# A transformer block on one core: own weight tiles for the last two blocks of the first feed-forward, no GpSimd work in the token mixers, and a re-ordered opening

## The chip, the core and the metric

The kernel runs on one core of a Trainium2 chip. The engines are named as in the profile: PE is TensorE (PEld its weight loads), DVE is VectorE, ACT is ScalarE, POOL is GpSimd, SP is SyncE, which here only issues DMAs. The metric is the device time of one execution in microseconds (us), the median over several runs; lower is better. About 0.2% (2 us) is the smallest change that a measurement of this kernel tells from none.

## What is computed

One layer over 256 latent tokens with 256 context tokens, width 1024, all in float32:

```python
mod = silu(c) @ w_ada + b_ada                  # 9 vectors of 1024 for x, and for ctx with c_ctx
x   = x   + 0.5 * g1x * swiglu(modulate(rmsnorm(x)), w13_ffn1, w2_ffn1)     # d_ff = 2816
ctx = ctx + 0.5 * g1c * swiglu(modulate(rmsnorm(ctx)), w13_ffn1, w2_ffn1)
qc, kc, vc, ...  = modulate(rmsnorm(ctx)) @ w_in
qx, kx, vx, g, f, ga, gf = modulate(rmsnorm(x)) @ w_in
o = bidirectional retention of x, started from the states of ctx             # 4 heads, rope on q, k
r = (silu(g) * (o - mean) * rsqrt(var + eps) * gn_w) @ p_ret
fo = real(fft2(f by groups of 256)) @ p_four
x = x + g2x * ((sigmoid(ga) * r + sigmoid(gf) * fo) @ w_out)
x = x + 0.5 * g3x * swiglu(modulate(rmsnorm(x)), w13_ffn2, w2_ffn2)
return rmsnorm(x)
```

## The kernel before

Data lie transposed: 8 tiles of 128 channels by 512 tokens (columns 0 to 255 are the context, 256 to 511 the latents), two to each of the `xs` tiles. To keep float32 accuracy, each operand of a product is split in a high part (rounded to fp32r) and a low part, and `mm3` (L95 to L97) makes three products: low weight by high data, high by low, high by high. A weight is therefore first loaded raw by a DMA on SP's queue (`wr`, four buffers), then cast by ACT (`wh`, L85), and subtracted by DVE or POOL (`wl`, L86), four buffers each. `load_w` does the three steps; its argument `lo_engine` chooses the engine of the subtraction. Four `t2k` buffers serve most temporaries; there are 8 PSUM banks.

The stages in order:

- The opening (L98 to L415), in an order written out by hand for PE, ACT, DVE and SP. Squares of `xs` are summed by products with a tile of ones (`st`, L257); ACT takes the square root (`sd1q`), DVE the reciprocal (`rstd1q`, L235), and four products with a pick matrix spread it over the partitions (`rs`, L269). DVE's `ada` (L198) makes one column of the modulation from an `ada` weight tile; PE makes another by transposing such a tile (`ada_turn`, L284), multiplying it (`ada_rows`, L295) and turning the row back (`ada_cols`, L306). Then the first three blocks of the up product run over 8 steps `k` (`first_products`), with `first_scaled`, `first_split` and `first_shifted` feeding them.
- The rest of the first feed-forward: `ffn1_up` and `ffn1_down` for two halves of the 22 blocks. In the second `ffn1_down` the last two output blocks, j = 6 and 7, are made for the context first (`y_6_0`, `y_7_0`) and then for the latents (`y_6_1`, `y_7_1`), so that the context's norm (`stage2_norm(0)`, `st_0`, `sd_0`, `rstd_0`) is under way while PE still works. Outside the opening the scheduler of the framework orders each engine's instructions.
- The mixers. `stage2_mod` makes the modulated `h2c` (context) and `h2x` (latents): per block a DVE product (`xr`, L328), an ACT addition with rounding (`h2ch`, L331), and a DVE subtraction (`h2cl`, L332). `first_unit` makes head 0's keys from them while PE transposes them (`ht`, L631); its `hook` starts the latents' norm behind block `HOOK`. Then for each of four heads: scores (`score_unit`), `u_unit`, `o_unit` (with the squares `os`, added on POOL at L757) and `o_norm`. The subtractions of `wk` and `wq` for head 0 and of the first four gate weights `wg` are on POOL.
- The gates: eight `gate_unit`s, with the Fourier branch between them (`fourier_tokens`: `fac`, `fbc`, `cu`; `fourier_channels`: `mx`). `o_norm` of the last head stands behind `gate_unit(1)`; its result, `tt` 6 and 7, is used by `gate_unit(6)` and `gate_unit(7)`.
- The merge, the output product, the second feed-forward and the last norm, which the change does not touch.

Of the kernel before, what the change touches and what calls it, by code (L numbers as in the profile page):

```python
# [13 lines left out]
P = 128  # L14
# [15 lines left out]
HOOK = 0  # L30
# [9 lines left out]
def block_kernel(ctx: ExitStack, tc: tile.TileContext, i: dict, out: bass.AP):  # L40
# [36 lines left out]
    def load_w(src, n, lo_engine=None, at=0):  # L77

        uid[0] += 1
        raw, hi, lo = [wtile(t, f"{t}{uid[0]}")[:, at : at + n] for t in ("wr", "wh", "wl")]  # L80
        dst = raw
        if len(src.shape) == 3:
            dst = dst.rearrange("p (k c) -> p k c", k=src.shape[1])
        nc.sync.dma_start(dst, src)
        S.copy(hi, raw)  # L85
        (lo_engine or V).tensor_tensor(lo, raw, f32(hi), op=ALU.subtract)  # L86
        return hi, lo
# [76 lines left out]
    nc.sync.dma_start(sm, i["smalls"])  # L164
# [76 lines left out]
    for k in range(KT):  # L241
        if k < T2K:
            sq = tp.tile([P, 512], F32, name=f"sq1_{k}", tag="t2k", bufs=T2K)
        else:
            sq = stp.tile([P, 512], F32, name=f"sq1_{k}", tag=f"at{k % 2}" if k < 6 else "xr", bufs=1 + (k > 5))
        if k % 2:
            V.tensor_tensor(sq, xs[k], xs[k], op=ALU.mult)
        else:
            S.activation(sq, xs[k], AF.Square)
        if k == 1:  # L250
            cb_copy(0, V.tensor_copy)
            cb_copy(1, S.copy)
        if k == 3:
            cb_copy(2, V.tensor_copy)
            cb_copy(3, S.copy)
        for q in range(4):
            PE.matmul(  # L257
                ps_st[32 * q : 32 * q + 32, :P], ones[:, :32], sq[:, q * P : (q + 1) * P],
                start=(k == 0), stop=(k == KT - 1), skip_group_check=True, tile_position=(0, 32 * q),
            )  # L260
    pick = stp.tile([P, 512], F32, name="pick")
    V.memset(pick, 0.0)
    for q in range(4):
        V.memset(pick[32 * q : 32 * q + 1, q * P : (q + 1) * P], 1.0)
    r1 = rstd_of(ps_st[:, :P], P, "1q")
    ps_st = bank("rs1")
    rstd1 = stp.tile([P, 512], F32, name="rstd1")
    for q in range(4):
        PE.matmul(  # L269
            ps_st[:, q * P : (q + 1) * P], pick[:, q * P : (q + 1) * P], r1, start=True, stop=True  # L270
        )
    for s in range(2):
        S.copy(rstd1[:, s * T : (s + 1) * T], ps_st[:, s * T : (s + 1) * T])

# [28 lines left out]
    def ada_cols(n):  # L303

        tr, row = turned.pop(n)
        PE.matmul(tr[0][:, :2], row, both, start=True, stop=True)  # L306
        V.tensor_scalar(
            mod[:, :, n : n + 1].rearrange("p s o -> p (s o)"), tr[0][:, :2],
            sm[:, BIAS + n : BIAS + n + 1], None, op0=ALU.add,
        )  # L310

# [44 lines left out]
    def first_split(k):  # L356
        hi, lo = wtile("wh", f"wh0_{k}"), wtile("wl", f"wl0_{k}")
        S.copy(hi[:, :n1], first_w[k][:, :n1])
        V.tensor_tensor(lo[:, :n1], first_w[k][:, :n1], f32(hi[:, :n1]), op=ALU.subtract)
        first_hl[k] = hi, lo  # L360
# [30 lines left out]
    ada_turn(0)  # L391
    first_scaled(0)
    first_split(0)
    ada_rows(0)
    ada_cols(0)
    first_shifted(0)
    acc = [bank(f"acc{m}") for m in range(2 * M1)]
# [45 lines left out]

    def w2_chunks(src, kts, at=0):
# [27 lines left out]
    def ffn1_down(hf, gs, n_ada=0):  # L472
# [3 lines left out]
        for j in range(KT):  # L476
            some_ada(n_ada)
            in_two = hf and j >= KT - 2
            ws = w2_chunks(i["w2a"][hf, j], (6, 5), 16 if in_two else 0)
            if in_two:  # L480
# [81 lines left out]
    nc.sync.dma_start(dist, i["dist"])  # L562
# [19 lines left out]
    nc.sync.dma_start(raw, i["unit"])  # L582
    V.tensor_copy(unit, raw)
    dec = {0: decays(0)}
    S.activation(warm, dec[0][0][:, :1], AF.Sqrt, bias=dec[0][1][:, :1])
    ffn1_down(1, g)
    ffn1.close()
# [104 lines left out]
    def k_weights(hd):  # L692
        return [load_w(i["wk"][hd, n], 1024, None if hd else G) for n in range(2)]
# [28 lines left out]
    def q_weights(hd):  # L722
        return [load_w(i["wq"][hd, n], 1024, None if hd else G) for n in range(2)]
# [21 lines left out]
    def o_unit(hd, us):  # L745
# [8 lines left out]
        sq = [tp.tile([P, 512], F32, name=f"os{hd}_{n}", tag="t2k", bufs=T2K) for n in range(2)]  # L754
        for d in range(4):
            S.activation(sq[d // 2][:, (d % 2) * T : (d % 2 + 1) * T], pss[d][:, :T], AF.Square)
        G.tensor_tensor(sq[0], sq[0], sq[1], op=ALU.add)  # L757
# [3 lines left out]
        return sq[0]  # L761
# [82 lines left out]
    def gate_unit(n):  # L844
        ws = [load_w(i["wg"][n, c], 1024, G if n < 4 else None) for c in range(2)]
# [48 lines left out]
    o_norm(HEADS - 1, sq)  # L894
# [10 lines left out]
    for n in range(5, KT):  # L905
        gate_unit(n)
# [260 lines left out]
```

## Time and profile before

| | |
|---|---|
| runs before | 989.15, 987.53, 987.61 us; median 987.61 |
| profiled execution | 986.11 us, of which the span from first to last instruction is 984.3 |
| granted TensorE clock, mean | 0.995 |
| PE busy | 957.3 us (97%) |
| DVE, ACT, POOL busy | 658.1 (67%), 468.1 (48%), 37.7 (4%) |
| subtractions of 128x1024 on DVE (L86) | 174, 1223 ns each |
| the same on POOL | 12, 2515 ns each |

A profile is one execution. In the timeline a row gives the start, the duration of the group of like instructions that follow each other, engine, line and operation, and in brackets the idle time of the engine ahead of it and what ended that. The table of windows gives the busy time of each engine in a stretch, with the number of instructions, the clock that PE was granted (1.00 is full), the share of the DMA engines and GB/s. A busy PE is not always a fast PE: the granted clock tells more.

### The profile page before, as it was taken

The page shows a single profiled execution, that of the slowest core. Times are in us where ns is not written, and L with a number is a line of the kernel's source. Part 1 is how long each engine was busy: PE and PEld are TensorE (multiplying, and loading weights), DVE is VectorE, ACT ScalarE, POOL GpSimd, SP SyncE. Part 2 cuts the span into 40 slices and gives each one's busy share as a digit, 9 for nine tenths or more (in the row PEclk, how much of TensorE's full clock was granted, in tenths as well). Part 3 has the DMA queues.
Part 4 walks back from the last instruction along what each step waited for, and adds up shares of the span by engine and source line. Part 5 has one row for each costly group of instructions (what it writes and reads, how often), then busy time and mean ns, then how long its engine had stood idle before and what let it go on. Part 6 is the DMA issues. An engine that isn't in the chain of part 4 may idle for free.

```text
span 984.3 us, 16732 instructions
## 1 busy us (share of the span) xinstructions
PE 957.3 (97%) x6792; PEld 881.2 (90%) x6792; DVE 658.1 (67%) x1056; ACT 468.1 (48%) x733; POOL 37.7 (4%) x21
## 2 busy tenths in 40 slices
PE   6999999999999999899999999899999999999996
PEld 4778888888888889899999999899999999999995
DVE  7879999998333433966765646975555688555553
ACT  5444322224422432755665647755444566555541
POOL 0000000000000001200000006200000000000000
PEclk9999999999999999999999999999999999999998
DMA  8757766995332232323231526356656565666661
GB/s 348 238 203 235 235 195 214 352 391 195 97 109 67 78 99 86 97 87 121 95 130 44 157 81 186 117 175 201 192 189 199 174 190 175 211 198 186 199 190 43
DMA packets 49237, 166.84 MB, mean 169 GB/s; under 512 B 5380, under 2 KB 7044, under 8 KB 49160
## 3 DMA queue, kind: packets, MB, share of 16 engines
q1 hardware_dynamic: 49160, 165.77, 52.4%
q8 instruction: 53, 0.87, 0.3%
q14 instruction: 24, 0.20, 0.1%
HBM read 164.70 MB, written 1.05 MB: 168 GB/s over the span
## 4 chain that ended last, share of the span: by engine, by line
PE 93%; DVE 3%; ACT 1%; DMA 1%; issue 1%; DVEq 0%; SPq 0%; ACTq 0%
PE y L95 4%; PE y L97 4%; PE y L96 4%; PE pa L97 4%; PE pb L95 4%; PE pa L95 4%; PE pb L97 4%; PE pa L96 3%; PE pb L96 3%; PE ro L97 2%; PE ro L95 2%; PE ro L96 2%; PE fb L97 2%; PE fa L97 2%; PE fb L96 2%; PE fa L96 2%
## 5 line engine op out<-in xcount | busy, mean ns | idle before, releaser
L86 DVE TENSOR_TENSOR wl<-wr,wh 128x1024 fp32r<-128x1024 f32 (+1 forms) x214 | 248.7, 1163 | 190.4 <-ACT wh L85 189.5
L85 ACT CAST wh<-wr 128x1024 fp32r<-128x1024 f32 (+1 forms) x226 | 227.3, 1007 | 273.7 <-PE y L97 79.2
L198 DVE CUSTOM_DVE_ANT_0 junk<-ada,cb,sm 128x1024 bf16<-128x1024 f32 x96 | 123.0, 1281 | 6.5 <-DMA ada<-in_ada 4.9
L96 PE MATMUL y<-gl,wh 128*128 128x512 f32 (+1 forms) x198 | 72.4, 366 | 0.0
L95 PE MATMUL y<-gh,wl 128*128 128x512 f32 (+1 forms) x198 | 72.3, 366 | 0.0
L97 PE MATMUL y<-gh,wh 128*128 128x512 f32 (+1 forms) x198 | 72.2, 365 | 0.0
L97 PE MATMUL pa<-h1h,wh 128*128 128x512 f32 x152 | 59.2, 389 | 0.0
L96 PE MATMUL pa<-h1l,wh 128*128 128x512 f32 x152 | 59.2, 389 | 0.0
L95 PE MATMUL pa<-h1h,wl 128*128 128x512 f32 x152 | 59.2, 389 | 0.0
L95 PE MATMUL pb<-h1h,wl 128*128 128x512 f32 x152 | 59.2, 389 | 0.0
L96 PE MATMUL pb<-h1l,wh 128*128 128x512 f32 x152 | 59.2, 389 | 0.0
L97 PE MATMUL pb<-h1h,wh 128*128 128x512 f32 x152 | 59.1, 389 | 0.0
L96 PE MATMUL z<-g2l,wh 128*128 128x256 f32 x176 | 48.8, 277 | 0.0
L97 PE MATMUL z<-g2h,wh 128*128 128x256 f32 x176 | 48.6, 276 | 0.0
L95 PE MATMUL z<-g2h,wl 128*128 128x256 f32 x176 | 48.6, 276 | 0.0
L86 POOL TENSOR_TENSOR wl<-wr,wh 128x1024 fp32r<-128x1024 f32 x12 | 29.9, 2515 | 439.2 <-ACT wh L85 439.2
L96 PEld LDWEIGHTS y<-gl,wh 128*128 128x128 f32 x198 | 37.3, 188 | 6.1
L95 PEld LDWEIGHTS y<-gh,wl 128*128 128x128 f32 x198 | 37.2, 188 | 6.0
L97 PEld LDWEIGHTS y<-gh,wh 128*128 128x128 f32 x198 | 37.2, 188 | 6.0
L97 PE MATMUL fb<-hnh,wh 128*128 128x256 f32 x144 | 39.8, 276 | 0.0
L96 PE MATMUL fb<-hnl,wh 128*128 128x256 f32 x144 | 39.8, 276 | 0.0
L97 PE MATMUL fa<-hnh,wh 128*128 128x256 f32 x144 | 39.8, 276 | 0.0
(336 smaller groups left out, 2903.1 us busy)
## 6 DMA issues: line engine op xcount, KB each, us to landing
ada<-in_ada SPq DMA_DIRECT2D x72, 512.0 KB, 5.2
wr<-in_w13b SPq DMA_DIRECT2D x44, 512.0 KB, 4.4
wr<-in_w13a SPq DMA_DIRECT2D x38, 512.0 KB, 4.4
wrv<-in_wv SPq DMA_DIRECT2D x16, 512.0 KB, 4.5
wr<-in_wg SPq DMA_DIRECT2D x16, 512.0 KB, 4.1
wr<-in_wgate SPq DMA_DIRECT2D x16, 512.0 KB, 4.4
wr<-in_pret SPq DMA_DIRECT2D x16, 512.0 KB, 4.1
wr<-in_w2b SPq DMA_DIRECT2D x16, 512.0 KB, 3.8
```

What stands on the lines that cost most here:

```text
L85: S.copy(hi, raw)
L86: (lo_engine or V).tensor_tensor(lo, raw, f32(hi), op=ALU.subtract)
L95: PE.matmul(o, w[1], a[0], start=start, stop=False)
L96: PE.matmul(o, w[0], a[1], start=False, stop=False)
L97: PE.matmul(o, w[0], a[0], start=False, stop=stop)
L198: V.tensor_tensor_reduce(junk, raw, cb[:, s, :], 1.0, sm[:, BIAS + n : BIAS + n + 1], ALU.mult, ALU.add, mod[:, s, n : n + 1],)
```

## The change

Four edits, by the places they touch:

1. In the second `ffn1_down`, blocks 6 and 7 get weight tiles of their own in a pool `late` (opened behind the modulation work, closed ahead of the mixers), no longer four pairs of the rotating `wh` and `wl`. The raw tiles still rotate through `wr`.
2. Nothing in the mixers is on POOL: the 12 subtractions and the 4 additions of `os` go to DVE. The last head's sum gets a tile that lives longer, and `o_norm` of the last head stands ahead of `gate_unit(6)`. `HOOK` is 1.
3. The opening: the second load of `unit` (used much later) is kept in its place in the program; `smalls` is loaded ahead of the `ada` tiles; for each step the tile that PE turns is loaded ahead of the one that DVE reduces; `ada_turn(0)` stands ahead of the spreading of `rstd1`; the first split is made in two pieces, around `first_shifted(0)`.
4. Products of `ones` with `ones` on PE ("constant products"): 5 ahead of the first transposes, and 1, 2 and 1 between the sums of squares. Their results are overwritten.

```diff
-HOOK = 0
+HOOK = 1
...
-    def load_w(src, n, lo_engine=None, at=0):
+    def load_w(src, n, at=0):
...
-        (lo_engine or V).tensor_tensor(lo, raw, f32(hi), op=ALU.subtract)
+        V.tensor_tensor(lo, raw, f32(hi), op=ALU.subtract)
...
+    nc.sync.dma_start(sm, i["smalls"])
     def first_loads(k):
-        for n in (KT + k, k):
+        for n in (k, KT + k):
...
     first_loads(0)
-    nc.sync.dma_start(sm, i["smalls"])
     first_loads(1)
...
+    def keep_warm(o, n):
+        for _ in range(n):
+            PE.matmul(o, ones, ones, start=True, stop=True, skip_group_check=True)
+    idle = ps
+    keep_warm(idle[:, :P], 5)
...
+        keep_warm(idle[:, :P], (0, 0, 1, 0, 2, 0, 1, 0)[k])
...
     r1 = rstd_of(ps_st[:, :P], P, "1q")
     ps_st = bank("rs1")
+    ada_turn(0)
...
-    ada_turn(0)
-    first_scaled(0)
-    first_split(0)
     ada_rows(0)
+    first_scaled(0)
     ada_cols(0)
+    first_split(0, 0, T)
     first_shifted(0)
+    first_split(0, T, n1)
...
+    def late_weights(src, j):
+        pair = [pools["late"].tile([P, HALF * P], F32R, name=f"late{j}_{x}") for x in range(2)]
+        for k0, k1 in ((0, 6), (6, HALF)):
+            c = slice(k0 * P, k1 * P)
+            uid[0] += 1
+            raw = wtile("wr", f"wr{uid[0]}")[:, : (k1 - k0) * P]
+            nc.sync.dma_start(raw, src[:, c])
+            split(pair[0][:, c], pair[1][:, c], raw)
+        return [sl(pair, slice(None), slice(k * P, (k + 1) * P)) for k in range(HALF)]
...
-            ws = w2_chunks(i["w2a"][hf, j], (6, 5), 16 if in_two else 0)
+            if hf and j >= KT - 2:
+                ws = late_weights(i["w2a"][hf, j], j)
+            else:
+                ws = w2_chunks(i["w2a"][hf, j], (6, 5))
...
-    nc.sync.dma_start(raw, i["unit"])
+    tc.keep_in_program_order(nc.sync.dma_start(raw, i["unit"]))
...
-        return [load_w(i["wk"][hd, n], 1024, None if hd else G) for n in range(2)]
+        return [load_w(i["wk"][hd, n], 1024) for n in range(2)]
...
-        G.tensor_tensor(sq[0], sq[0], sq[1], op=ALU.add)
+        V.tensor_tensor(sums, sq[0], sq[1], op=ALU.add)
...
-        ws = [load_w(i["wg"][n, c], 1024, G if n < 4 else None) for c in range(2)]
+        ws = [load_w(i["wg"][n, c], 1024) for c in range(2)]
...
-    o_norm(HEADS - 1, sq)
     fourier_tokens(1)
...
     for n in range(5, KT):
+        if n == 2 * (HEADS - 1):
+            o_norm(HEADS - 1, sq)
         gate_unit(n)
```

How the instructions stand, at three places. First PE in the opening, from the last sum of squares on, before:

```order
L257 MATMUL st_153<-sq_7_200,ones 32x128 x4
L269 MATMUL rs_216<-rstd1q,pick 128x128 x4
L284 MATMUL tr_0_240<-unit_raw,ada_116 128x128 x4
L284 MATMUL tr_1_241<-unit_raw,ada_116 128x128 x4
L295 MATMUL tr_1_241<-at_0_242,ct 32x128 x4
```

and with the change:

```order
L266 MATMUL st_158<-sq_7_209,ones 32x128 x4
L279 MATMUL tr_0_226<-unit_raw,ada_115 128x128 x4
L279 MATMUL tr_1_227<-unit_raw,ada_115 128x128 x4
L316 MATMUL rs_225<-rstd1q,pick 128x128 x4
L290 MATMUL tr_1_227<-at_0_228,ct 32x128 x4
```

The eight transposes of the first `ada` tile (`tr`) now stand between the sum of squares (`st`) and the products that spread its reciprocal (`rs`).

Second, DVE at the end of the first feed-forward, where `xs<-y_4` and so on take up the output blocks; before:

```order
L86 TENSOR_TENSOR wl_3171<-wr_3169,wh_3170 128x768
L467 SCALAR_TENSOR_TENSOR xs_110<-y_5_3118,gate,xs_110 128x256 x2
L86 TENSOR_TENSOR wl_3177<-wr_3175,wh_3176 128x640
L462 TENSOR_TENSOR ssum_2851<-ssum_2851,sq_5_3154 128x512
L467 SCALAR_TENSOR_TENSOR xs_112<-y_6_0_3181,gate,xs_112 128x256
```

and with the change:

```order
L91 TENSOR_TENSOR late_1_3184<-wr_3189,late_0_3183 128x640
L483 TENSOR_TENSOR ssum_2867<-ssum_2867,sq_3_3068 128x512
L86 TENSOR_TENSOR wl_3425<-wr_3423,wh_3424 128x1024
L488 SCALAR_TENSOR_TENSOR xs_110<-y_4_3083,gate,xs_110 128x256 x2
L86 TENSOR_TENSOR wl_3431<-wr_3429,wh_3430 128x1024
L483 TENSOR_TENSOR ssum_2867<-ssum_2867,sq_4_3119 128x512
L86 TENSOR_TENSOR wl_3721<-wr_3719,wh_3720 128x1024
L488 SCALAR_TENSOR_TENSOR xs_110<-y_5_3134,gate,xs_110 128x256 x2
L86 TENSOR_TENSOR wl_3727<-wr_3725,wh_3726 128x1024
L483 TENSOR_TENSOR ssum_2867<-ssum_2867,sq_5_3170 128x512
L488 SCALAR_TENSOR_TENSOR xs_112<-y_6_0_3193,gate,xs_112 128x256
```

The last pieces of blocks 6 and 7 (`late`) are subtracted during block 3, and the four subtractions of head 0's `wk` and `wq` (the 128x1024 rows, which POOL made before) during blocks 4 and 5, ahead of the first output of block 6.

Third, DVE at the start of the gates (`dft` is the Fourier matrix, `fbl` and `fu` its input, `sg` a gate), before:

```order
L64 MEMSET pad_cu 128x80
L91 TENSOR_TENSOR dft_5374<-dftr_5375,dft_5373 128x384
L91 TENSOR_TENSOR dft_5374<-dftr_5379,dft_5373 128x384
L798 TENSOR_TENSOR fbl_1_5512<-fal_5506,f_1_5481 128x512
L91 TENSOR_TENSOR fu_0_1_5386<-fbl_0_5508,fu_0_0_5385 128x512
L798 TENSOR_TENSOR fbl_0_5709<-fal_5707,f_1_5682 128x512
L798 TENSOR_TENSOR fbl_1_5713<-fal_5707,f_1_5682 128x512
L91 TENSOR_TENSOR fu_1_1_5388<-fbl_1_5512,fu_1_0_5387 128x512
```

and with the change:

```order
L86 TENSOR_TENSOR wl_5983<-wr_5981,wh_5982 128x1024
L64 MEMSET pad_dft 128x80
L64 MEMSET pad_fu 128x96
L64 MEMSET pad_cu 128x80
L91 TENSOR_TENSOR dft_5387<-dftr_5388,dft_5386 128x384
L91 TENSOR_TENSOR dft_5387<-dftr_5392,dft_5386 128x384
L828 TENSOR_TENSOR fbl_1_5525<-fal_5519,f_1_5494 128x512
L91 TENSOR_TENSOR fu_0_1_5399<-fbl_0_5521,fu_0_0_5398 128x512
L86 TENSOR_TENSOR wl_5989<-wr_5987,wh_5988 128x1024
L828 TENSOR_TENSOR fbl_0_5722<-fal_5720,f_1_5695 128x512
L828 TENSOR_TENSOR fbl_1_5726<-fal_5720,f_1_5695 128x512
L91 TENSOR_TENSOR fu_1_1_5401<-fbl_1_5525,fu_1_0_5400 128x512
```

Three subtractions of gate weights now stand ahead of the Fourier matrix (the last of them is the first row here), one between the two `fu` rows, and the other four behind.

More of the change, by code (lines that the diff above doesn't have):

```diff
@@ L260, in block_kernel @@
             )
[L261 to L273, printed above, removed]
     turned = {}
@@ L310, in ada_cols @@
         )
+    pick = stp.tile([P, 512], F32, name="pick")
+    V.memset(pick, 0.0)
+    for q in range(4):
+        V.memset(pick[32 * q : 32 * q + 1, q * P : (q + 1) * P], 1.0)
+    r1 = rstd_of(ps_st[:, :P], P, "1q")
+    ps_st = bank("rs1")
+    ada_turn(0)
+    rstd1 = stp.tile([P, 512], F32, name="rstd1")
+    for q in range(4):
+        PE.matmul(
+            ps_st[:, q * P : (q + 1) * P], pick[:, q * P : (q + 1) * P], r1, start=True, stop=True
+        )
+    for s in range(2):
+        S.copy(rstd1[:, s * T : (s + 1) * T], ps_st[:, s * T : (s + 1) * T])
     def modulated(dst, st, s, k, rstd, col, name, engine=None, lo=None):
@@ L354, in block_kernel, with first_split @@
     first_hl = {}
[L356 to L360, printed above, removed]
+    def first_split(k, c0=0, c1=n1):
+        if k not in first_hl:
+            first_hl[k] = wtile("wh", f"wh0_{k}"), wtile("wl", f"wl0_{k}")
+        c = slice(c0, c1)
+        split(first_hl[k][0][:, c], first_hl[k][1][:, c], first_w[k][:, c])
     xr1 = {}
@@ L477, in ffn1_down @@
             some_ada(n_ada)
-            in_two = hf and j >= KT - 2
-            ws = w2_chunks(i["w2a"][hf, j], (6, 5), 16 if in_two else 0)
-            if in_two:
+            if hf and j >= KT - 2:
+                ws = late_weights(i["w2a"][hf, j], j)
+            else:
+                ws = w2_chunks(i["w2a"][hf, j], (6, 5))
+            if hf and j >= KT - 2:
                 late.append((j, ws))
@@ L561, in block_kernel @@
     dist = dp.tile([P, 512], F32, name="dist")
-    nc.sync.dma_start(dist, i["dist"])
+    tc.keep_in_program_order(nc.sync.dma_start(dist, i["dist"]))
     def decays(hd):
@@ L585, in block_kernel @@
     S.activation(warm, dec[0][0][:, :1], AF.Sqrt, bias=dec[0][1][:, :1])
+    late = ExitStack()
+    pools["late"] = fpool(late, "late", "left")
+    shifted(pools["late"], "pad_late", 10)
     ffn1_down(1, g)
+    late.close()
     ffn1.close()
@@ L722, in q_weights @@
     def q_weights(hd):
-        return [load_w(i["wq"][hd, n], 1024, None if hd else G) for n in range(2)]
+        return [load_w(i["wq"][hd, n], 1024) for n in range(2)]
     def project(ws, a, name):
@@ L754, in o_unit @@
         sq = [tp.tile([P, 512], F32, name=f"os{hd}_{n}", tag="t2k", bufs=T2K) for n in range(2)]
+        sums = sq[0]
+        if hd == HEADS - 1:
+            sums = per.tile([P, 512], F32, name="ssum_o", tag="ssum")
         for d in range(4):
             S.activation(sq[d // 2][:, (d % 2) * T : (d % 2 + 1) * T], pss[d][:, :T], AF.Square)
-        G.tensor_tensor(sq[0], sq[0], sq[1], op=ALU.add)
+        V.tensor_tensor(sums, sq[0], sq[1], op=ALU.add)
         for d in range(4):
@@ L760, in o_unit @@
             S.copy(tt[2 * hd + d // 2][:, c], pss[d][:, :T])
-        return sq[0]
+        return sums
     def o_norm(hd, sq):
```

2 lines of the change are left out of this document (1 added, 1 removed).

## The prediction, as it was put on record

> **What bounds the kernel now.** First I read the page's slices and then the windows (length; PE, PEld, DVE, ACT, POOL busy; granted clock; DMA share; GB/s).
>
> ```profile
> PE   6999999999999999899999999899999999999996
> POOL 0000000000000001200000006200000000000000
> 0.00:20.00 20.00, 10.96 (x119) 7.03 (x119) 14.42 (x36) 11.48 (x22) 0.20 (x4) 1.00 0.86 333
> 395.59:411.32 15.73, 12.11 (x87) 11.27 (x87) 15.33 (x29) 9.06 (x20) 5.01 (x3) 0.89 0.41 131
> 401.00:402.00 1.00, 1.00 (x6) 0.91 (x5) 1.00 (x2) 0.01 (x1) 1.00 (x1) 0.50 0.24 90
> 590.00:600.00 10.00, 10.00 (x88) 10.00 (x87) 4.62 (x11) 7.74 (x14) 4.99 (x3) 1.00 0.77 236
> 600.00:610.00 10.00, 9.15 (x77) 8.78 (x76) 9.65 (x9) 6.37 (x14) 7.17 (x3) 1.00 0.56 181
> 610.00:620.00 10.00, 7.74 (x62) 7.24 (x61) 7.20 (x8) 8.71 (x14) 7.59 (x5) 1.00 0.37 107
> 620.00:630.00 10.00, 9.02 (x75) 8.81 (x76) 10.00 (x13) 7.00 (x11) 2.10 (x1) 1.00 0.32 105
> 630.00:640.00 10.00, 10.00 (x90) 10.00 (x89) 10.00 (x15) 7.56 (x12) 0.00 (x0) 1.00 0.49 136
> ```
>
> PE is the bound nearly everywhere, so no edit gains where PE is full: no product of the kernel goes away. It dips at the opening, near 400 us and near 610 us, and the last two dips are where POOL works. What can be had: in the middle PE is idle for 15.73 − 12.11 = 3.62 us and loses another (1 − 0.89) × 15.73 = 1.73 us to a lower granted clock (0.50 for some us from 401); in the gates, 600 to 630, it is idle for 30 − 25.91 = 4.09 us. The last slice is the end, which the change leaves alone.
>
> Then I read the timeline of the middle: what PE waits for, and what DVE and POOL do meanwhile.
>
> ```profile
> 395.31 0.28 PE L97 MATMUL y<-gh,wh 128*128 128x256 f32 x1
> 396.60 0.47 PE L95 MATMUL kc<-h2ch,wl 128*128 128x256 f32 x2 [1.02 <-ACT h2ch L331]
> 399.01 0.68 PE L631 MATMUL ht<-unit,h2ch 128*128 128x128 f32 x2 [1.88 <-ACT h2ch L331]
> 400.30 0.38 PE L96 MATMUL kc<-h2cl,wh 128*128 128x256 f32 x1 [0.61 <-DVE h2cl L332]
> 390.87 7.26 POOL L86 TENSOR_TENSOR wl<-wr,wh 128x1024 fp32r<-128x1024 f32 x3 [390.43 <-ACT wh L85]
> 393.44 5.77 DVE L328 SCALAR_TENSOR_TENSOR xr<-xs,amul,rstd 128x256 f32<-128x256 f32 x4
> 399.13 0.47 DVE L467 SCALAR_TENSOR_TENSOR xs<-y,gate,xs 128x256 f32<-128x256 f32 x1
> 399.82 1.22 DVE L332 SCALAR_TENSOR_TENSOR h2cl<-xr,mod,h2ch 128x256 fp32r<-128x256 f32 x3
> 407.06 1.74 DVE L235 RECIPROCAL rstd<-sd 128x256 f32<-128x256 f32 x1
> 408.84 1.67 DVE L328 SCALAR_TENSOR_TENSOR xr<-xs,amul,rstd 128x256 f32<-128x256 f32 x4
> ```
>
> Four `xr` take 5.77 us while POOL subtracts from 390.87 to 398.1, and 1.67 us at 408.84, when POOL is idle. PE's three waits all hang on these rows: `h2ch` and `h2cl` are made from `xr`. So in this trace a POOL instruction does not take work off DVE; it stretches it, by 4.10 us here.
>
> The gates' timeline says the same:
>
> ```profile
> 605.84 0.38 PE L95 MATMUL sq<-dft,fu 128*128 128x256 f32 x1 [0.53 <-DVE fu L91]
> 617.41 0.39 PE L95 MATMUL mx<-cu,dft 128*128 128x256 f32 x1 [1.64 <-ACT cu L90]
> 622.70 0.39 PE L96 MATMUL mx<-cu,dft 128*128 128x256 f32 x1 [0.98 <-DVE cu L91]
> 595.01 10.22 POOL L86 TENSOR_TENSOR wl<-wr,wh 128x1024 fp32r<-128x1024 f32 x4 [40.87 <-ACT wh L85]
> 616.92 5.18 POOL L86 TENSOR_TENSOR wl<-wr,wh 128x1024 fp32r<-128x1024 f32 x2 [2.41 <-ACT wh L85]
> 599.72 3.24 DVE L91 TENSOR_TENSOR dft<-dftr,dft 128x384 fp32r<-128x384 f32 x2 [4.50 <-ACT dft L90]
> 603.49 2.30 DVE L91 TENSOR_TENSOR fu<-fbl,fu 128x512 fp32r<-128x512 f32 x1
> 617.39 5.26 DVE L91 TENSOR_TENSOR cu<-fbc,cu 128x512 fp32r<-128x512 f32 x2
> 628.57 1.28 DVE L91 TENSOR_TENSOR cu<-fbc,cu 128x512 fp32r<-128x512 f32 x2
> L86 DVE TENSOR_TENSOR wl<-wr,wh 128x1024 fp32r<-128x1024 f32 x174 | 212.6, 1223 | 154.3 <-ACT wh L85 153.6
> ```
>
> Two `cu` take 5.26 us beside POOL and 1.28 alone, so 0.64 per 128x512. Against that price, `dft` (about 0.96 for two of 128x384) loses 2.28, the first `fu` 1.66, `cu` 3.98: 7.92 us in the quoted rows alone. The last row is what a subtraction costs on DVE: 1.22 us.
>
> **The change part by part: the middle.** Four subtractions, 4 × 1.22 = 4.9 us, go to DVE, ahead of the first output of block 6. The own tiles are what allows that: the four pairs of `wh` and `wl` are no longer held by blocks 6 and 7. PE works without a pause there, so DVE does them under PE. Then `xr` costs 1.67 instead of 5.77, and the context's chain ends more than 4 us earlier, before y's last product (395.31 + 0.28 = 395.59). What is late next: block 7's update of the latents (0.47), the pads (estimate 0.3) and one `h2cl` (0.41) still follow that product, so `h2cl` is there near 396.8, while the first keys' products that need no `h2cl` last about 0.4. I leave a pause of 0.9. The latents' norm, moved one block later, has its reciprocal (1.74) and `xr` (1.67) end near 405.3, by a start of its sums near 400; the latents' keys would now begin near 411.32 − 4.4 = 406.9, so it is covered by 1.6 us; past that each us costs one. Gain 3.62 + 1.73 − 0.9 = **4.45**, with the clock's 1.73 included because the long run of waits that precedes the 0.50 is gone. Bounds: 2.7 (the clock's part stays: 3.62 − 0.9) and 5.35 (no pause).
>
> The late pieces are loaded, cast and subtracted in turn behind earlier weights, in the order ACT and DVE take them. By my walk the last piece of block 6 is ready near 371 and needed near 375; this is an estimate from the subtraction's 1.22 and PE's rate, and the cover is some 4 us.
>
> **The gates.** Eight subtractions come to DVE: 9.8 us, and the long rows shrink by at least 7.92. Three of the eight stand ahead of `dft`, in 590 to 600, where DVE is busy for 4.62 of 10 us; they fit. The other five, 6.1 us, go against the 7.92 freed. Walking DVE's order: third subtraction ends near 600.4, `dft` 601.5, first `fu` 602.7; PE wants it at 605.84 − 0.53 = 605.3. The last `fu` is cast by ACT near 605.6. That brings forward ACT's own long stretch, which is next in line:
>
> ```profile
> 608.41 0.65 ACT L756 ACTIVATE os<-o 128x256 f32<-128x256 f32 x2
> 613.45 0.58 ACT L795 COPY fac<-sq 128x512 f32<-128x512 f32 x1
> 469.14 0.69 DVE L742 TENSOR_TENSOR sc<-s,dec 128x512 f32<-128x512 f32 x1 [1.89 <-PE s L97]
> ```
>
> From `os` at 608.41 to `fac` at 614.03 ACT is occupied for 5.6 us; 2.8 earlier it ends near 611.2, and `cu` is cast near 613.2, about 1 us before PE, freed of its 0.85 us of earlier waits, arrives. So nearly all of 4.09 goes; I take **3.7**, since a margin of 1 us may not hold at each of the later `cu`. Bounds 2.0 (the subtractions behind `fu` meet `cu` and half the idle time stays) and 4.1. `o_norm` moves to where gate 6 begins: its work is the same, and DVE and ACT have room there. The adds of `os` cost DVE 0.64 per head; for the first three heads the next DVE row, `sc`, waits 1.89 for PE, which hides it.
>
> **The opening.** DVE paces it (14.42 of 20) and DMA is nearly saturated (0.86).
>
> ```profile
> 1.19 0.41 SPq L582 DMA_DIRECT2D unit<-in_unit  x1
> 10.69 1.08 PE L257 MATMUL st<-sq,ones 128*32 128x128 f32 x16 [0.19 <-ACT sq L249]
> 11.32 0.85 DVE L264 MEMSET pick<- 1x128 f32 x4
> 12.23 0.95 DVE L235 RECIPROCAL rstd1q<-sd1q 128x128 f32<-128x128 f32 x1
> 13.75 1.28 DVE L198 CUSTOM_DVE_ANT_0 junk<-ada,cb,sm 128x1024 bf16<-128x1024 f32 x1 [0.57 <-DMA sm<-in_smalls]
> 16.11 0.65 PE L295 MATMUL tr<-at,ct 128*32 128x128 f32 x16 [0.84 <-ACT at L287]
> ```
>
> The second `unit` load (0.41 of issue) no longer stands ahead of `xs`, so all that follows is about 0.4 earlier; `sm` in front removes 0.57 of waiting at 13.75. Together up to 0.98; I take **0.8**, as the split in two pieces puts its second one behind `h1h` on ACT. Bounds 0.2 (the constant products, two of which fill more than the pause they stand in, push the last `st`) and 1.2. The constant products themselves I cost at nothing: they lie in pauses of PE, and the chain through `st` is met at 12.17 by DVE's memsets, 0.06 before the reciprocal starts.
>
> Sixteen `st` take 1.08 and sixteen `tr` of the same tiles 0.65, though the clock's column reads 1.00 for this stretch. The Trainium skill, page TensorE: Matmul & The Clock Gate (section on the HAM clock gate), says that PE starts at half clock and is released after some 3.4 us of sustained work. By that rule the constant products would save up to 1.08 − 0.65 = 0.43 more, and the time would be 978.2 instead of 978.7; the memsets speak against it.
>
> **Sum.** 0.8 + 4.45 + 3.7 = 8.95 off the profiled 986.11. That execution is 1.5 below the median of the runs, 987.61; the stages' differences carry over, so the forecast is 987.61 − 8.95 = **978.7**.
>
> **Rivals.** *The clock drops all the same.* The remaining pause of 0.9 lets the half clock come: 1.73 lost again, 980.4. Against it: the pause of 1.64 at 617.41 left its window at 1.00. The same page says that one idle window of about 3.4 us brings the half clock, which a pause of 0.9 would not fill. Chance 0.07.
>
> *DVE has no room in the gates.* It is busy for 10.00 of 10 from 620 to 640. If what POOL gave back is spent on the subtractions among `cu`, the gain there is 0: 982.4. Against it: 7.92 freed and 6.1 put in. Chance 0.05.
>
> *Slower: the long rows are not POOL's doing.* If `xr`, `fu` and `cu` are long because of their own place (many operands, transfers beside them), they stay long, DVE, full already, gets five subtractions and an addition more, 6.1 + 0.64 = 6.8 us, in front of PE, and the middle gains nothing: 987.61 − 0.8 + 6.8 = 993.6. It decides if `cu` and `fu` stay above about 1.3 each with POOL idle. The Trainium skill, page Perfetto Trace Analysis, section Optimizing Scalar/DVE Operations, bears on this: with DVE saturated, handing work to another engine, even GpSimd, may pay, and this change does the reverse; it adds that the two share a read port, so that it might not. The equal shapes at 408.84 and 628.57, each with POOL idle, speak against this rival. Chance 0.02.
>
> *The late tiles come too late.* If the last pieces come 13 us later than I walked them, the 4 us of cover are gone and PE waits for 9: all three gains are spent, 987.6. Against it: each piece waits for a handful of subtractions of 1.22, not for ten of them. Chance 0.02.
>
> **How the numbers follow.** The forecast's own case has 0.84. The range takes in the terms' bounds: 987.61 − (1.2 + 5.35 + 4.1) − 0.43 = 976.5 and 987.61 − (0.2 + 2.7 + 2.0) = 982.7, which holds the first two rivals as well. Faster by over 0.2% (2 us, about what a measurement can tell): 0.84 + 0.07 + 0.05 = 0.96; within 0.2%: 0.02, slower: 0.02.
>
> **What would show it right or wrong.** In the profile after: POOL nearly at 0; no `xr` x4 above 2 us; from y's last product to the latents' first keys about 11.3 us instead of 15.73, at a clock near 1.00; PE idle for under 0.5 us in the gates; the first `ada` on DVE near 12.9 instead of 13.75. It is wrong if a wait of PE on `late` tiles appears before 395, if PE waits for `cu` with DVE busy at 128x1024 rows, or if `fu` rows stay at 2 us.

## The result, and the profile after

The changed kernel takes 975.96 us (median of 4 runs, 975.41 to 976.15), the kernel before 987.57 beside it: a ratio of 0.9874, 95% interval 0.9862 to 0.9886. It is faster, as forecast, but by 11.6 us where 8.95 were forecast, and the time lies 0.5 below the range. The profiled execution took 975.8, its span 974.0.

The busy slices of the page after, PE and POOL:

```profile
PE   8999999999999999999999999999999999999996
POOL 0000000000000000000000000000000000000000
```

Both dips in the middle of the program are gone. The windows after, the first from y's last product to the latents' first keys (columns as before: length; PE, PEld, DVE, ACT, POOL; clock; DMA share; GB/s):

```profile
395.45:406.56 11.11, 10.51 (x90) 10.01 (x88) 9.84 (x25) 8.18 (x19) 0.00 (x0) 1.00 0.01 2
600.00:610.00 10.00, 9.83 (x87) 9.64 (x86) 8.73 (x13) 9.97 (x20) 0.00 (x0) 1.00 0.46 153
610.00:620.00 10.00, 10.00 (x88) 10.00 (x87) 10.00 (x17) 6.47 (x12) 0.00 (x0) 1.00 0.50 159
620.00:630.00 10.00, 10.00 (x88) 10.00 (x86) 9.33 (x15) 6.97 (x11) 0.00 (x0) 1.00 0.50 154
```

and the same stretch of the kernel before, measured between the same two starts:

```profile
395.31:411.32 16.01, 12.39 (x90) 11.35 (x88) 15.61 (x29) 9.06 (x20) 5.29 (x3) 0.89 0.42 134
```

The same 90 products take 16.01 us before and 11.11 after: 4.9 gained. In the gates look at the counts, not at the busy time: 87, 88 and 88 products in three windows where the kernel before had 77, 62 and 75.

The timeline of the middle, after:

```profile
396.33 0.51 PE L95 MATMUL kc<-h2ch,wl 128*128 128x256 f32 x2 [0.60 <-ACT h2ch L341]
...
406.56 0.48 PE L95 MATMUL kx<-h2xh,wl 128*128 128x256 f32 x2
376.81 1.22 DVE L86 TENSOR_TENSOR wl<-wr,wh 128x1024 fp32r<-128x1024 f32 x1 [2.25 <-ACT wh L85]
393.58 1.67 DVE L338 SCALAR_TENSOR_TENSOR xr<-xs,amul,rstd 128x256 f32<-128x256 f32 x4
402.27 1.75 DVE L243 RECIPROCAL rstd<-sd 128x256 f32<-128x256 f32 x1 [0.37 <-ACT sd L241]
```

One pause of 0.60 is left of three that made 3.51; `xr` is at 1.67, and the latents' reciprocal ends at 404.0, early enough. The opening, after:

```profile
12.13 0.65 PE L266 MATMUL st<-sq,ones 128*32 128x128 f32 x16
13.25 0.95 DVE L243 RECIPROCAL rstd1q<-sd1q 128x128 f32<-128x128 f32 x1 [0.81 <-ACT sd1q L241]
14.12 1.19 DVE L206 CUSTOM_DVE_ANT_0 junk<-ada,cb,sm 128x1024 bf16<-128x1024 f32 x1
17.02 0.88 DVE L381 SCALAR_TENSOR_TENSOR xr<-xs,amul,rstd 128x256 f32<-128x256 f32 x2
17.95 0.42 DVE L91 TENSOR_TENSOR wl<-w,wh 128x256 fp32r<-128x256 f32 x1
18.61 0.88 DVE L391 SCALAR_TENSOR_TENSOR h1l<-xr,mod,h1h 128x256 fp32r<-128x256 f32 x2 [0.25 <-ACT h1h L388]
19.52 0.69 DVE L91 TENSOR_TENSOR wl<-w,wh 128x512 fp32r<-128x512 f32 x1
25.50 0.88 DVE L391 SCALAR_TENSOR_TENSOR h1l<-xr,mod,h1h 128x256 fp32r<-128x256 f32 x2 [0.58 <-ACT h1h L388]
```

and before:

```profile
16.75 0.88 DVE L371 SCALAR_TENSOR_TENSOR xr<-xs,amul,rstd 128x256 f32<-128x256 f32 x2
17.55 0.95 DVE L359 TENSOR_TENSOR wl<-w,wh 128x768 fp32r<-128x768 f32 x1
19.21 0.88 DVE L381 SCALAR_TENSOR_TENSOR h1l<-xr,mod,h1h 128x256 fp32r<-128x256 f32 x2 [0.58 <-ACT h1h L378]
```

Here the profile shows no gain. The last `st` starts at 12.13 (10.69 before), the reciprocal waits 0.81 for it, and the first `xr` is 0.27 later. The first `h1l` is still 0.6 earlier, because only one piece of the split stands ahead of it (0.42 in place of 0.95) and its wait for ACT is shorter (0.25 in place of 0.58). But the second piece (0.69) stands behind it, and the second `h1l` is 0.1 later (25.39 before).

Starts of the first or last product of a stage give the gain stage by stage, against the profile before that the prediction used and against a second one, taken later (run e8 below):

| stage | forecast | first profile of before | second profile of before |
|---|---|---|---|
| up to y's last product (opening) | 0.8 | -0.1 | 1.3 |
| to the latents' first keys | 4.45 | 4.9 | 5.9 |
| to the first `ro` product (gates) | 3.7 | 5.2 | 5.1 |
| to the second feed-forward | 0 | 0.4 | 0.4 |
| sum | 8.95 | 10.4 | 12.7 |

The kernel before takes 986.1 to 990.4 in its runs, and the two profiles are from that spread; the changed kernel's four runs differ by 0.7. So there were three things to explain: why the gates gained more than PE's idle time, where the 0.4 ahead of the second feed-forward comes from, and why the kernel before is usually slower than its first profile.

### The profile page after: what moved, and what is told of

The parts are those of the page before. It is cut to its first block, busy times and chain, and to the rows that moved or that the text cites. A ratio compares the mean times of both kernels' runs of the same rounds, so it can differ in the third digit from the quotient of the medians.

```text
span 974.0 us, 16757 instructions
## 1 busy us (share of the span) xinstructions
PE 958.0 (98%) x6810; PEld 882.6 (91%) x6810; DVE 657.4 (67%) x1074; ACT 468.1 (48%) x734; POOL 2.2 (0%) x5
## 4 chain that ended last, share of the span: by engine, by line
PE 96%; ACT 1%; DVE 1%; DMA 0%; issue 0%; DVEq 0%; SPq 0%; ACTq 0%
PE y L95 4%; PE y L97 4%; PE y L96 4%; PE pa L95 4%; PE pb L95 4%; PE pa L97 4%; PE pb L97 4%; PE pa L96 4%; PE pb L96 4%; PE ro L97 2%; PE ro L95 2%; PE ro L96 2%; PE fa L95 2%; PE fb L95 2%; PE fa L97 2%; PE fb L97 2%
## 5 line engine op out<-in xcount | busy, mean ns | idle before, releaser
L86 DVE TENSOR_TENSOR wl<-wr,wh 128x1024 fp32r<-128x1024 f32 (+1 forms) x222 | 259.8, 1172 | 186.7 <-ACT wh L85 186.1
L85 ACT CAST wh<-wr 128x1024 fp32r<-128x1024 f32 (+1 forms) x222 | 224.3, 1012 | 264.6 <-PE y L97 67.1
L96 PE MATMUL y<-gl,wh 128*128 128x512 f32 x154 | 59.9, 389 | 0.0
L97 PE MATMUL y<-gh,wh 128*128 128x512 f32 x154 | 59.9, 389 | 0.0
L95 PE MATMUL y<-gh,wl 128*128 128x512 f32 x154 | 59.7, 389 | 0.0
L95 PE MATMUL fb<-hnh,wl 128*128 128x256 f32 x144 | 39.7, 276 | 0.0
L95 PE MATMUL fa<-hnh,wl 128*128 128x256 f32 x144 | 39.6, 276 | 0.0
L96 PE MATMUL fa<-hnl,wh 128*128 128x256 f32 x144 | 39.6, 276 | 0.0
L354 ACT ACTIVATE sa<-pa 128x512 f32<-128x512 f32 x19 | 11.4, 599 | 56.7 <-PE pa L97 56.7
```

What stands on the lines that cost most here:

```text
L86: V.tensor_tensor(lo, raw, f32(hi), op=ALU.subtract)
L95: PE.matmul(o, w[1], a[0], start=start, stop=False)
L96: PE.matmul(o, w[0], a[1], start=False, stop=False)
L97: PE.matmul(o, w[0], a[0], start=False, stop=stop)
L354: S.activation(sa, pa, AF.Silu)
```

## The experiments

**e1: DVE for POOL, nothing else.** From the kernel before:

```
-        return [load_w(i["wk"][hd, n], 1024, None if hd else G) for n in range(2)]
+        return [load_w(i["wk"][hd, n], 1024) for n in range(2)]
-        return [load_w(i["wq"][hd, n], 1024, None if hd else G) for n in range(2)]
+        return [load_w(i["wq"][hd, n], 1024) for n in range(2)]
-        ws = [load_w(i["wg"][n, c], 1024, G if n < 4 else None) for c in range(2)]
+        ws = [load_w(i["wg"][n, c], 1024) for c in range(2)]
-        G.tensor_tensor(sq[0], sq[0], sq[1], op=ALU.add)
+        V.tensor_tensor(sq[0], sq[0], sq[1], op=ALU.add)
```

> The kernel before with one edit: the 12 subtractions and the 4 additions that POOL made go to DVE; the late blocks keep their rotating tiles, opening, HOOK and o_norm are those of before (987.6). Theory 1 (POOL stretches DVE's rows where the two coincide): the gates gain nearly all that the whole change gained there by its landmarks (5.3 us between the last f product and the first ro product), and the middle gains little, because without the own tiles the four subtractions of head 0 stand on DVE among the xr rows, 4 x 1.22 = 4.9 us in place of a stretch of about 5: 982.3, with the xr rows at 0.42 each. Theory 2 (the rows are long in their own right and the gain is the own tiles' and the order's): no gain or some us slower, 987.6 to 993, xr x4 near 5.8 and cu x2 near 5.3 still.

Measured: 989.23 against 988.64, ratio 1.0003 (0.9994 to 1.0012): no gain. The time is where theory 2 put it, yet the long rows are gone, as theory 1 has it. Middle and a later window:

```profile
396.97:414.01 17.04, 13.77 (x89) 12.60 (x88) 16.51 (x39) 10.39 (x24) 0.00 (x0) 0.80 0.34 109
396.72 1.67 DVE L328 SCALAR_TENSOR_TENSOR xr<-xs,amul,rstd 128x256 f32<-128x256 f32 x4
398.31 1.22 DVE L86 TENSOR_TENSOR wl<-wr,wh 128x1024 fp32r<-128x1024 f32 x1
401.76 0.58 PE L96 MATMUL kc<-h2cl,wh 128*128 128x256 f32 x1 [1.48 <-DVE h2cl L332]
620.00:630.00 10.00, 8.70 (x74) 8.50 (x73) 10.00 (x17) 7.44 (x12) 0.00 (x0) 1.00 0.43 118
700.00:710.00 10.00, 10.00 (x87) 10.00 (x86) 5.16 (x7) 4.93 (x6) 0.00 (x0) 1.00 0.54 171
```

Four `xr` take 1.67, so they were long because of POOL's work. But without the own tiles two of the four subtractions now stand between `xr` and `h2cl` (the one at 398.31 and one at 400.13), and the middle takes 17.04 us at a clock of 0.80, more than before. In the gates most waits go (one window of 8.70 is left). The last row was not expected by either theory: in 700 to 710 PE is full, has no wait, and makes 87 products, where the kernel before makes 91.

**e2: the own tiles, nothing else.** From the kernel before, `late_weights` and the pool `late` as in the change; POOL keeps all its work.

> The kernel before with one edit: blocks 6 and 7 of the first feed-forward get tiles of their own; POOL keeps its 12 subtractions and 4 additions. Theory 1: the own tiles let POOL subtract head 0's weights before block 6's first output, where no DVE row is waited for, so the middle gains as in the whole change (y's last product to the latents' keys 11.1 us in place of 16.0, 4.9 gained) although POOL does the work, and the gates gain nothing: 982.7. Theory 2 (only DVE in place of POOL helps, wherever it stands): no gain in the middle, 987.6.

Measured: 984.48 (982.78 to 984.91), ratio 0.9955 (0.9942 to 0.9967).

```profile
382.12 2.40 POOL L86 TENSOR_TENSOR wl<-wr,wh 128x1024 fp32r<-128x1024 f32 x1 [1.01 <-ACT wh L85]
395.44 1.66 DVE L328 SCALAR_TENSOR_TENSOR xr<-xs,amul,rstd 128x256 f32<-128x256 f32 x4
408.44 0.48 PE L95 MATMUL kx<-h2xh,wl 128*128 128x256 f32 x2
614.44 0.39 PE L95 MATMUL mx<-cu,dft 128*128 128x256 f32 x1 [1.64 <-ACT cu L90]
```

POOL ends its last subtraction at 384.5, eleven us ahead of `xr`, which takes 1.66. From y's last product (397.31) to `kx` are 11.13 us, as in the changed kernel. So the middle is cured by the tiles, which let the subtractions be early; which engine makes them doesn't matter there. In the gates the wait of 1.64 is what it was. Theory 1 holds in both places; the time is 1.8 above its 982.7, and the opening of this profile ends 2.0 later than in the first one of the kernel before.

**e3: both, with the old opening, `HOOK` 0 and `o_norm` in its old place.** The edits of e1 and e2 together.

> The kernel before with both edits (own tiles and everything of the mixers on DVE), without the new opening, HOOK 0 and o_norm behind gate_unit(1). If these two edits are the whole gain, as the landmarks of the changed kernel say (4.9 in the middle, 5.3 in the gates, opening 0.2 lost): 987.6 - 10.2 = 977.4 less the 0.4 and the 1.3 by which the runs of the two kernels differ beyond their profiles, so 975.8 to 977.4. If o_norm's new place or HOOK carries part of the gates' or the middle's gain: 978.5 to 980, with a wait of PE on cu or on h2xh left.

Measured: 983.78 (983.73 to 985.29), ratio 0.9956 (0.9944 to 0.9969): nothing above e2, although the first `ro` starts at 659.7 where it starts at 663.5 in e2. Both cases of the expectation missed. The windows show where the 4 us of the gates are lost again:

```profile
610.00:620.00 10.00, 8.68 (x76) 8.48 (x74) 10.00 (x15) 9.05 (x12) 0.00 (x0) 1.00 0.30 105
630.00:640.00 10.00, 10.00 (x88) 10.00 (x87) 8.57 (x14) 5.46 (x8) 0.00 (x0) 1.00 0.36 111
700.00:710.00 10.00, 10.00 (x87) 10.00 (x87) 4.67 (x4) 4.68 (x5) 0.00 (x0) 1.00 0.60 182
```

From 638 to 790 there are 87 or 88 products in every 10 us, not 91. (In 610 to 620 PE also waits once, 1.32 us for `cu`, while DVE is busy throughout.) The starts in the timeline lie 0.1178 apart in place of 0.1133: 3.8% over some 150 us, 5.7 us. PE is busy throughout and the granted clock reads 1.00. The same spacing is found in every kernel here from about 430 to 465 (in e10 only up to its break), in shorter stretches elsewhere, and in the kernel before from 780.7 to the second feed-forward. There the changed kernel has the narrow one: this is the row of 0.4 in the table.

**e4: the changed kernel without constant products.**

```
-    keep_warm(idle[:, :P], 5)
-        keep_warm(idle[:, :P], (0, 0, 1, 0, 2, 0, 1, 0)[k])
```

> The changed kernel without the constant products on PE. Theory A (they delay the chain: in the changed kernel the last st starts at 12.13 where it started at 10.69, and DVE's reciprocal waits 0.81 for it): the last st starts near 11.0 at 1.08, the reciprocal near 12.4 in place of 13.25, and the time falls by 0.8 to 1.0, to 975.1. Theory B (the clock that they bring forward pays for them): 976.0 or up to 0.4 slower. Theory C (DVE and the transfers pace the eight steps, so that an earlier start is waited away): 976.0 with the reciprocal earlier and h1l of the second step still at 25.5.

Measured: 975.79 (975.47 to 975.87) against 975.96 of the changed kernel: no difference that can be told. What A and B name is there in the profile:

```profile
12.08 1.97 PE L277 MATMUL tr<-unit_raw,ada 128*128 128x128 f32 x8
12.62 0.95 DVE L242 RECIPROCAL rstd1q<-sd1q 128x128 f32<-128x128 f32 x1
18.00 0.88 DVE L389 SCALAR_TENSOR_TENSOR h1l<-xr,mod,h1h 128x256 fp32r<-128x256 f32 x2 [0.24 <-ACT h1h L386]
```

The reciprocal is 0.6 earlier, and so is `h1l`, although eight transposes take 1.97 where they take 1.09 after the constant products. Of the 0.6, some 0.5 are still there at the last `ro` product (759.3 and 759.7), and 0.4 of that goes from 770 on, where this profile has the wide spacing and the changed kernel's has not. That the constant products cost these 0.6 is not shown: in e7, which has them, the first `h1l` starts at 17.88, earlier than the 18.00 here.

**e5: e3 with `o_norm` moved.** As in the change:

```
-    o_norm(HEADS - 1, sq)
     fourier_tokens(1)
...
     for n in range(5, KT):
+        if n == 2 * (HEADS - 1):
+            o_norm(HEADS - 1, sq)
         gate_unit(n)
```

with the sum of `os` in a tile that lives until then.

> The kernel before with own tiles, DVE for POOL and o_norm of the last head ahead of gate_unit(6) (run e3 plus that one move). In e3 the gates' waits are gone, but from 638 to 790 its 256-wide products follow each other at 0.1178 in place of 0.1133, 0.38 us lost in each 10. Theory S (a state of PE's issue that begins where its stream of products is disturbed and ends at the next break of another kind): o_norm's full-precision products at gate 6 end it, and the time falls from 983.8 by the 5.7 lost there and by some of the 1.0 that the changed kernel has less of waits in the gates: 977.1 to 978.2. Theory O (o_norm's old place costs nothing, and the wide spacing comes with DVE's subtractions): 983.8, spacing 0.1178 to 790 as before.

Measured: 978.06 (977.47 to 979.22), ratio 0.9895 (0.9881 to 0.9908), 5.7 below e3.

```profile
640.98 1.02 PE L786 MATMUL ov<-ssum_o,ones_dv 128*128 128x256 f32 x4
670.00:680.00 10.00, 10.00 (x91) 10.00 (x90) 4.91 (x4) 4.70 (x5) 0.00 (x0) 1.00 0.59 187
```

`ov`, products in full precision, now stand at 641, and the windows from 650 on have 91 products. Theory O fails; that products in full precision end the wide spacing is what e6, e10 and e11 test. Added up from the starts in the timeline, the wide spacing costs 5.7 us from 640 to 790 in e3 and 0.1 in e5, and what waits and spacing together cost from 600 to 640 falls from 2.8 to 1.4 us.

**e6: e3 with a break.** Ahead of the first `ro` product:

```
+        if j == 0:
+            pr = bank("reset")
+            for _ in range(4):
+                PE.matmul(pr[:, :P], ones, ones, start=True, stop=True)
```

> Run e3 with one thing added: four products of ones with ones, 128 wide and in full precision, on PE between the first merge gate and the first ro product, into a bank of their own that nothing reads. They cost about 0.5 to 1 us of PE. Theory S: they end the wide spacing there, about 660, so that some 130 of the 152 us run at 0.1133 again: 983.8 - 5.0 + 0.7 = 979.5. If the spacing comes from the addresses of the tiles or from the other engines' traffic, four products change nothing: 984.4.

Measured: 980.57 (978.87 to 981.6), ratio 0.9917 (0.9904 to 0.9931), 3.2 below e3 by the medians, 4.9 by the spans of the profiles (982.0 and 977.1).

```profile
640.00:650.00 10.00, 10.00 (x87) 10.00 (x87) 7.20 (x10) 6.41 (x8) 0.00 (x0) 1.00 0.52 150
658.65 1.05 PE L937 MATMUL reset<-ones 128*128 128x128 f32 x8
670.00:680.00 10.00, 10.00 (x91) 10.00 (x90) 4.35 (x6) 4.69 (x5) 0.00 (x0) 1.00 0.62 179
```

Work that nobody needs makes the kernel faster: 87 products in 10 us ahead of the break, 91 behind it, with the same tiles, stages and neighbours as e3.

**e7: the opening alone.** Parts 3 and 4 of the change on the kernel before; the load of `dist` is kept in its place in the program like that of `unit`.

> The kernel before with the new opening alone (order of loads, ada_turn, split in two, constant products, program order of the unit load). By the two profiles of before and after it loses 0.1 to the last product of the opening (73.2 to 73.3). Theory P (profile of before was a lucky one): in e1 to e3, with the opening of before, the last product starts at 74.4 to 75.2 because PE's clock rises some 7 us later, so against timed runs the new opening gains 1.2 to 2.0: 986.8 to 987.4 against 988.6, and the last product at 73.3 or below. Theory Q (the opening is worth nothing): 988.6.

Measured: 986.71 (985.88 to 987.58) against 988.2, ratio 0.9982 (0.9973 to 0.9991): 1.5 gained, and a narrower spread. Theory P holds: by the start of the last `acc` product the opening ends at 72.6 to 73.9 in the six profiles that have the new one, and in the seven with the old one twice at 73.2 and 73.5, five times at 74.4 to 75.2. The reason is in e8.

**e8: the kernel before once more.**

> The kernel before, unchanged, for a second profile. If its timed runs are longer than the first profile because of the opening's clock, the spreading products rs take 1.9 and the last product of the opening starts at 74.4 to 75.2; if because of the middle, the stretch at half clock near 401 is longer than 3.4; if because of the spacing of the products behind the gates, 0.38 are lost in each 10 us of some stretch between 640 and 790.

Measured: 988.42 (986.1 to 990.0), ratio 1.0; the profiled execution took 988.48, 2.4 more than the first one. In the second profile:

```profile
13.82 2.08 PE L269 MATMUL rs<-rstd1q,pick 128*128 128x128 f32 x8 [1.48 <-DVE rstd1q L235]
400.00:410.00 10.00, 8.93 (x48) 8.15 (x49) 9.25 (x20) 6.16 (x13) 2.48 (x1) 0.66 0.34 111
```

and in the first:

```profile
13.24 1.16 PE L269 MATMUL rs<-rstd1q,pick 128*128 128x128 f32 x8 [1.48 <-DVE rstd1q L235]
400.00:410.00 10.00, 9.70 (x68) 9.29 (x69) 9.60 (x16) 5.88 (x13) 2.47 (x1) 0.83 0.28 93
```

The same instructions on PE take 2.08 or 1.16 in the opening, and near 405 the clock is 0.66 or 0.83: about 7 us at half clock, or 3.4. By the starts of the stages that is 1.5 and 1.0 us. The first profile caught the good case in both. In e7, the third profile with the middle of before, half clock lasts 6.8 us as well, and the stage takes 17.3.

The Trainium skill, page TensorE: Matmul & The Clock Gate (section on the HAM clock gate), says that PE's clock is set by how busy it was in a window of about 3.4 us that runs freely, so that the same kernel warms up earlier or later from run to run. The two profiles agree: one more window in the middle, and an opening that depends on the run.

**e9: the changed kernel with the gates' subtractions back on POOL.**

```
-        ws = [load_w(i["wg"][n, c], 1024) for c in range(2)]
+        ws = [load_w(i["wg"][n, c], 1024, G if n < 4 else None) for c in range(2)]
```

> The changed kernel with the eight subtractions of the first four gates back on POOL, all else as changed (o_norm at gate 6, sum of os on DVE). Theory 1 (POOL's subtractions stretch DVE's dft, fu and cu, and PE waits for these): 4 us of PE's waits come back between 600 and 630, as in the kernel before and in e2 (6.8 lost from 590 to 640 against 1.9), 979.5 to 981, and dft x2 takes near 3.2, cu x2 near 5. Rival (the waits there were o_norm's work in the way, not POOL's): 976 to 977, with the long DVE rows no longer waited for.

Measured: 982.7 (980.56 to 983.22), ratio 0.9938 (0.9925 to 0.9952), 6.7 above the changed kernel.

```profile
595.47 3.24 DVE L91 TENSOR_TENSOR dft<-dftr,dft 128x384 fp32r<-128x384 f32 x2 [4.49 <-ACT dft L90]
612.73 5.24 DVE L91 TENSOR_TENSOR cu<-fbc,cu 128x512 fp32r<-128x512 f32 x2 [0.41 <-ACT cu L90]
612.75 0.39 PE L95 MATMUL mx<-cu,dft 128*128 128x256 f32 x1 [2.17 <-ACT cu L90]
613.00:616.00 3.00, 3.00 (x17) 3.00 (x17) 3.00 (x2) 2.13 (x4) 2.91 (x2) 0.56 0.17 19
```

Only the engine of eight subtractions differs, and the long rows are back (3.24 and 5.24; 3.24 and 5.26 in the kernel before): POOL is their cause. PE waits 2.17 in one place, and behind that wait its clock falls to half, which makes the price larger than the waits and than theory 1's 979.5 to 981. The Trainium skill, page Perfetto Trace Analysis, section Optimizing Scalar/DVE Operations, says that handing work of a saturated DVE to another engine, even GpSimd, may pay, and adds that it might not, because the two share a read port. Here it cost 6.7 us; that the port is the reason, no run here shows.

**e10: the changed kernel with a break**, where all kernels have the wide spacing, ahead of the first `u_unit`:

```
+        if hd == 0:
+            pr = bank("reset")
+            for _ in range(2):
+                PE.matmul(pr[:, :P], ones, ones, start=True, stop=True)
         us = u_unit(hd)
```

> The changed kernel with two full-precision products of ones with ones on PE between the keys of head 1 (kc) and the first u product, into a bank that nothing reads. In the changed kernel the products stand 0.1178 apart from 428 to 463. Theory S (such products end that state): from about 435 on the spacing is 0.1133, 28 us x 3.8% = 1.1 gained less about 0.25 to 0.4 for the two products: 975.2. If the state returns at once at the next disturbance (u and q products are mixed there): 976.2 to 976.4.

Measured: 975.07 (975.00 to 975.18), ratio 0.9868 (0.9854 to 0.9881).

**e11: the same break in the rounded type**, `unit` with `unit` in place of `ones` with `ones`.

> Run e10 with one difference: the two products between kc and u are of unit with unit in the rounded type (one pass each, as all the large products have) instead of ones with ones in full precision. If any foreign product ends the wide spacing: as e10, 975.1, with 0.1133 apart from 435 to 463. If it takes the full precision (several passes): 976.0, with 0.1178 apart until 463 as in the changed kernel.

Measured: 976.29 (975.61 to 976.83), ratio 0.9875 (0.9853 to 0.9896). The window 440 to 450 of e10:

```profile
440.00:450.00 10.00, 10.00 (x91) 10.00 (x90) 4.11 (x7) 3.14 (x7) 0.00 (x0) 1.00 0.33 107
```

and of e11:

```profile
440.00:450.00 10.00, 10.00 (x87) 10.00 (x87) 4.08 (x7) 2.79 (x7) 0.00 (x0) 1.00 0.32 107
```

At the same place two products in full precision end the wide spacing and two in the rounded type do not. The changed kernel has 87 products in this window too. In the stage with the break, from the latents' first keys to the last product of `f`, e10 gains 0.5 on the changed kernel. The two rounded products are also over sooner (0.17 us against 0.37); whether their type or their length matters was not separated. e10 is the fastest version here; its runs lie below all of the changed kernel's (975.41 and up), though the two were not timed side by side.

## Why the prediction was wrong in size

- **The middle** (4.45 forecast, 4.9 to 5.9): right in mechanism. The pause left is 0.60 where 0.9 was allowed, which is 0.3 of the 0.45 missing against the first profile, and the clock stays at 1.00. Against the second profile the term is short by 1.5, because the half clock lasts 6.8 us there, as in e7, and not 3.4. The part given to DVE for POOL was not needed: e2 has the whole gain with POOL. Nor was the later `HOOK`: e5 has 0 and takes the same 11.11.
- **The gates** (3.7 forecast, 5.1 to 5.2): the step that failed is the bound "PE is idle for 30 − 25.91 = 4.09". A busy PE of the profile hides losses: its 62 products in 610 to 620, against 90 at full rate in 630 to 640, say more than its 7.74 us busy. The page lets a product end 0.28 us after its start, though the next one follows after 0.1133, so each wait costs more than the idle time shown. By the starts, the five waits behind the 4.09 cost 4.9, and the one that is left (0.17, at 608.26) costs 0.3. The other 0.6 of the gain is spacing: wide or irregular spacing costs 2.5 us in this stage before and 1.9 after. That POOL is the cause of the long rows is shown by e9. That DVE has room holds with `o_norm` in its new place only: in e3 PE still waits 1.32 for `cu` beside a full DVE. The one wait that is left:

```profile
608.26 0.38 PE L95 MATMUL mx<-cu,dft 128*128 128x256 f32 x1 [0.17 <-ACT cu L90]
```

- **"`o_norm` moves to where gate 6 begins: its work is the same"**: so it is, but by e3 and e5 its place is worth 5.7 us. Without the move, e3 gives back the gates' gain behind them. That the two edits come together in the change is the forecast's luck.
- **The opening** (0.8 forecast, -0.1 to 1.3): the size is fair, by luck; the terms were wrong. The wait of 0.57 for `sm` is gone, but the first `ada` on DVE stands at 14.12, not near 12.9, behind a reciprocal that is 1.0 later. What the first `h1l` gains is the split's, and the second piece, named but not costed, takes it back. The constant products were costed at nothing. What they cost the chain is not settled (e4 against e7); what they seem to bring is the clock: in the traces' clock records full clock is first on record at 12.6 us or earlier in all five profiles with them (in e9 and e11 it falls back for a while before 23), and at 11.7 to 22.8 in the eight without. The prediction's "the clock's column reads 1.00" rests on no record: in the first profile the first one stands at 11.65, behind the start of the last `st`. Against the runs the opening gains 1.5 (e7). Which of its parts does that was not separated; the one profile of e4 ends its opening at 72.7 without the constant products, the best of those with them at 72.6.
- **"The stages' differences carry over" from the profiled 986.11 to the median 987.61** is the step that put the time outside the range. With the stages as the first profile has them, 10.4 in all, the sum would have been 977.2, inside the range. But the 1.5 between the profile and the median was no offset common to both kernels: it was clock lost in the opening and the middle, which the change removes. Carried over from the starts of the stages the gain is 10.4 from the good profile and 12.7 from the second; the runs show 11.6.
- Of the rivals, none came in the changed kernel; the second came in part in e3. The half clock that the first one feared is real: e9 shows it behind a wait of 2.17, the kernel before has none behind 1.64, and the changed kernel has no wait above 0.60 there.

What stays open: why the wide spacing begins. It is seen to begin where PE's order of products is broken or after a short wait, and not at every such place. It also ends at places without products in full precision, as among the scores (`s`) at 463 in the changed kernel.

## What to carry to other kernels

Count a full engine's instructions per window: PE at 10.00 of 10 made 87 or 91 products, and at 7.74 lost more than its idle time. Before a profile is used as the base of a sum, take a second one when the runs spread more than the sum's terms; what differs between them is often what the change removes. And a helper engine is free only where the engine that it slows has nothing on the path: here that was a question of when POOL ran, and own buffers moved it.

## What the runs showed of the hardware

- PE has two spacings of its 256-wide rounded products, 0.1133 and 0.1178 us, at a granted clock of 1.00 in both. The wide one lasted over 150 us (e3) through several stages, and ended at products in full precision (e5, e6, e10), not at two rounded ones (e11). These are not its only ends.
- Beside two POOL subtractions of 128x1024, two DVE subtractions of 128x512 take 5.24 in place of 1.28 (e9). That is 3.96 more, where DVE needs 2 × 1.22 to make both POOL rows itself.
- The half clock came behind a single wait of 2.17 us on PE (e9), with full work ahead of it and behind. The Trainium skill, page TensorE: Matmul & The Clock Gate (section on the HAM clock gate), names an idle window of about 3.4 us for it; here PE was not idle for the whole of one. In these traces the clock changes in steps of 3.41 us. Behind the opening, every step at full clock with up to 1.24 us of PE work was followed by half clock, and none with 1.81 or more. These two are the step with that wait in e9, and in the kernel before the step with the wait of 1.64:

```profile
609.93:613.34 3.41, 1.24 (x11) 1.04 (x10) 3.00 (x6) 2.73 (x5) 1.08 (x1) 1.00 0.50 154
615.81:619.22 3.41, 1.81 (x14) 1.69 (x14) 3.21 (x3) 3.41 (x6) 2.30 (x1) 1.00 0.35 139
```
